# The output projection as seven half-size products instead of eight

## The chip, the cores and the metric

The kernel runs on one core of a Trainium2 chip. The metric is the device time of one execution in microseconds (us). Below, PE is TensorE (matrix products), DVE is VectorE, ACT is ScalarE, POOL is GpSimd and SP is SyncE, which only issues transfers. Each engine works through its own queue in program order; PSUM is the memory that TensorE accumulates into, SBUF the working memory of all engines, DRAM the memory outside.

## The reference

One decoder block on x of 1024 rows by 1024 columns, in float32. Cut to what matters here:

```python
o_a = swa_sink_attention(qa, ka, va, swa_sinks[l])     # sliding window, 8 heads
o_b = mla_attention(q_nope, q_rope, k_nope, k_rope, vb) # causal, 8 heads
y = jax.nn.sigmoid(g_a) * (o_a @ w_o_swa[l]) + jax.nn.sigmoid(g_b) * (o_b @ w_o_mla[l])
x = x + y @ w_out[l]
h = rmsnorm(x, ffn_norm_g[l])
x = x + (jax.nn.silu(h @ w_gate[l]) * (h @ w_up[l])) @ w_down[l]
return rmsnorm(x, final_norm_g)
```

The change concerns `y @ w_out`: 1024x1024 by 1024x1024, with the mixing that makes y ahead of it and the norm and the feed-forward part behind.

## The kernel before

Every float32 operand of a product is split into a rounded upper half and a lower half (`split`, L163 the cast on ScalarE, L166 the subtraction on VectorE), and `mm3` (L172 to L174) makes three matmuls of them: upper by upper, upper by lower, lower by upper. One matmul has a 128x128 stationary tile and 512 columns.

Order of the stages: projections of the input with the sliding-window attention beside them (the gate stage, in which the gates' products run as filler), the second attention, the mixing, the out projection, the feed-forward part, the last norm.

**Mixing.** y is made transposed, in eight bands `dc` of 128 columns, in the order of `DCS`. ScalarE takes the sigmoids of two gates (L1269), GpSimd multiplies the first with the first mixer's projection `ar` (L1434), in two halves of 128x512. TensorE makes the second mixer's projection oB in two halves `sh` (12 matmuls each, one PSUM bank of four of the pool `PX`). VectorE multiplies it with the second gate straight from PSUM (L1420), which frees the bank, adds the two (L180) and splits the sum (`yh` from ScalarE, `yl` from VectorE). All 16 halves are split and stay as `y`. The bands 0 to 3 of `ar` wait in DRAM (`ar_d`). The tile scheduler sets the order here, within the order in which the code was written.

**Out projection.** Four segments (row half `sh`, column half `hf`): (0,0), (0,1), (1,1), (1,0), each of four blocks of 128 rows. One block in one segment is one `xo`: eight bands by three matmuls in a bank of the other PSUM pool `P1`. VectorE adds it to x (L180). The weights come as units of 512 KB ("out", r, j), loaded by SP (L238), split by ScalarE and VectorE; half 0 is loaded and split twice, 12 units in all. After both column halves of a block: Square on ScalarE (L1644), `rstd` on GpSimd (L311, L314), the norm on VectorE (L1649), the block to DRAM, and `to_h`, which transposes it on TensorE and lowers it for the feed-forward part (for blocks 4 to 7 the second half of that, `rest`, is called later). From the last segment on, the order on TensorE, VectorE, ScalarE and GpSimd is that of the code (`manual_schedule`); before, the scheduler's.

**Feed-forward part.** It already works with seven products in place of eight (class `Seven`), its sums made by GpSimd and VectorE. It starts with `ffn.run()`, after loads and sums called `load_part`, `mix` and `prep_to`.

**The gate stage**, where part of the change stands, is a loop of 16 steps; in each GpSimd normalises the sliding window's weights `pe` (L935 to L938), and its loads go through SP.

Of the kernel before, what the change touches and what calls it, by code (L numbers as in the profile page):

```python
# [89 lines left out]
def hybrid_block_kernel(  # L90
# [208 lines left out]
    for dp in range(4):  # L299
        plain(("oa", dp), w_o_swa[dp], (P, 4, 256), True)  # L300
    for dp in (2, 0, 3, 1):
        plain(("ob", dp), w_o_mla[dp], (P, 4, 256))
    OUT0 = (2, 0, 3, 1)
    for r, hf in enumerate((0, 1, 0)):
        for j in (range(4) if r else OUT0):
            plain(("out", r, j), w_out[hf, j], (P, 2, 512), (r, j) != (2, 3))
# [718 lines left out]
    for it in range(N_SW):  # L1025
        if it + 2 < N_SW:
            sw_q(it + 2)
        gate_step()
        if it + 1 < N_SW:
            sw_qT(it + 1)  # L1030
        gate_step()
        if it >= 1:
            sw_pv(it - 1)
        if it + 1 < N_SW:
            sw_scores(it + 1)
        if it == N_SW - 1:
            load_lat(4)
        gate_step()
        sw_pT(it)
# [236 lines left out]
    def mix_a(dc, sh, c0, n, ps=None):  # L1276
        if ps is not None:
            oa_ps[(dc, sh)] = ps
        ps = oa_ps[(dc, sh)]
        if (sh, c0) == (0, 0):  # L1280
            if dc < 4:
                ar[dc] = U("ar")
            elif dc % 2 == 0:
                t = V("ar", F32, (P, 2, S))
                ar[dc], ar[dc + 1] = t[:, 0], t[:, 1]
            if dc % 2 == 0:
                wo[dc // 2] = st.get(("oa", dc // 2))
        w = wo[dc // 2]
        mm3(ps, [((w[0][:, c, blk(dc % 2)], w[1][:, c, blk(dc % 2)]), oaT[(c, sh)]) for c in range(c0, c0 + n)],
            c0 == 0, c0 + n == 4)  # L1290
        if c0 + n == 4:
            nc.scalar.copy(ar[dc][:, half(sh)], oa_ps.pop((dc, sh)))
            if sh == 1 and dc < 4:
                nc.sync.dma_start(ar_d[dc], ar.pop(dc))
# [16 lines left out]
    DCS = (4, 5, 0, 1, 6, 7, 2, 3)  # L1311

    def load_sigs(dc):
        for i in (dc, 8 + dc):
            load_sig(i)
        if dc < 4:
            ar[dc] = U("ar")
            nc.sync.dma_start(ar[dc], ar_d[dc])
# [35 lines left out]
    units = [(u // 2, u % 2, c) for u in range(16 - 3) for c in (0, 2)]  # L1354
# [5 lines left out]
    for t in range(NT):  # L1360
# [20 lines left out]
        if t == NT - 1:  # L1381
            mix_a(13 // 2, 13 % 2, 0, 4, PX("oA"))
# [7 lines left out]
        if t + 6 in w_at or t == 0:  # L1390
            st.load_to(st.index[("oa", w_at.get(t + 6, 0))])
# [6 lines left out]
        if e in (2, 6):  # L1398
            st.load_to(st.index[("ob", 2 if e == 2 else 0)])
        if e == 6:  # L1400
            st.conv_to(st.index[("ob", 2)])
        held[0] = False
    rest = [(i // 2, i % 2) for i in range(14, 16)]
# [6 lines left out]

    def mix_b(dc, i):
# [3 lines left out]
        ga, gb = gate.pop(dc), gate.pop(8 + dc)  # L1415
        for sh in range(2):
# [4 lines left out]
            if i == 7:  # L1421
                add(ga[:, cs], ga[:, cs], gb[:, cs], nc.vector)
                split(*hT(dc, cs), ga[:, cs])
        for sh in range(2 if i < 7 else 0):
            cs = half(sh)
            add(ga[:, cs], ga[:, cs], gb[:, cs], nc.vector)
            split(*hT(dc, cs), ga[:, cs])
# [14 lines left out]
    st.conv_to(st.index[("ob", 0)])  # L1442
    new_quads("y")
    for i, dc in enumerate(DCS):
        if i in (1, 2):
            st.load_to(st.index[("ob", (3, 1)[i - 1])])
        if 2 <= i < 6:
            st.load_to(st.index[("out", 0, OUT0[i - 2])])
# [4 lines left out]
        if i + 1 < 8:  # L1453
            sigmoids(DCS[i + 1])
        mix_b(dc, i)
        if i in (1, 3):
            st.conv_to(st.index[("ob", (3, 1)[i // 2])])
        if i >= 4:
            st.conv_to(st.index[("out", 0, OUT0[i - 4])])

# [3 lines left out]
    x2 = {}  # L1464
# [3 lines left out]
    def to_h(xn, b):  # L1468
# [3 lines left out]
        for kh in range(2):  # L1472
            ps = PX("tp", (P, 4, P))
# [133 lines left out]

    in_order = tc.manual_schedule(engines={engines.PE, engines.DVE, engines.Activation, engines.Pool})
    prev = None
    late_parts = []  # L1610
    for seg, (sh, hf) in enumerate(((0, 0), (0, 1), (1, 1), (1, 0))):
        if seg == 3:
            in_order.__enter__()
        if seg in (0, 1, 3):
            r = {0: 0, 1: 1, 3: 2}[seg]
            wo2 = [st.get(("out", r, j)) for j in range(4)]
        hs = half(hf)
        for b in range(4 * sh, 4 * sh + 4):
            if seg in (0, 2):
                x2[b] = load_x(b)  # L1620
            if (seg, b) == (2, 4):
                ffn.load_part(0, 0)
            if (seg, b) == (2, 6):
                ffn.load_part(0, 1)
            if (seg, b) == (2, 7):
                ffn.mix(0)
            if seg == 0 and b < 2:
                if b == 0:
                    xo2 = [P1("xo") for _ in range(2)]
                    for ks in (DCS[:6], DCS[6:]):  # L1630
                        for u in range(2):
                            mm3(xo2[u], [(hT(k, blk(u)), (wo2[k // 2][0][:, k % 2], wo2[k // 2][1][:, k % 2])) for k in ks],
                                ks[0] == DCS[0], ks[0] != DCS[0])
                ps = xo2[b]
            else:
                ps = P1("xo")
                mm3(ps, [(hT(k, blk(b)), (wo2[k // 2][0][:, k % 2], wo2[k // 2][1][:, k % 2])) for k in DCS])
            add(x2[b][:, hs], ps, x2[b][:, hs], nc.vector)
            if seg in (0, 2):
                st.conv_to(st.index[("out", seg // 2 + 1, b % 4)])  # L1640
            if seg in (1, 3):
                xn = U("xn")
                ss = tiny("ss")
                nc.scalar.activation(xn, x2[b], AF.Square, accum_out=ss)  # L1644
                rs = rstd_of(ss, D)
            lower = to_h(*prev) if prev is not None else None
            prev = None
            if seg in (1, 3):
                nc.vector.scalar_tensor_tensor(xn, x2[b], rs, fg_bc, op0=ALU.mult, op1=ALU.mult)  # L1649
                prev = (xn, b)  # L1650
                if (seg, b) == (3, 6):
                    ffn.prep_to(3)
                nc.sync.dma_start(x2_d[b], x2.pop(b))
            if (seg, b) == (3, 7):
                for kh in range(2):
                    ffn.load_part(1, kh)
            if lower is not None:
                if seg == 3 and b >= 6:
                    late_parts.append(lower)
                else:  # L1660
                    lower()
    ffn.n_ahead = 1
    ffn.run()
    late_parts.pop(0)()
    ffn.run()
    ffn.prep_to(5)
    late_parts.pop(0)()
    ffn.run()
    ffn.prep_to(6)
    lower = to_h(*prev)  # L1670
    ffn.run()
    ffn.run()
    ffn.prep_to(7)
    lower()
# [210 lines left out]
```

## Time and profile before

| | |
|---|---|
| median of 3 runs | 1340.86 us (1339.17 to 1341.85) |
| profiled execution | 1340.2 us, its span 1338.4 us |
| TensorE clock granted | 0.998 |
| TensorE busy | 1325.0 us (99%) |
| VectorE, ScalarE, GpSimd busy | 904.0 (68%), 635.5 (47%), 566.9 us (42%) |
| oB of the mixing on TensorE | from 563.9 us on |
| out projection on TensorE | 607.4 to 699.7 us |

Rows are read as: start, duration, engine, line, operation, output<-inputs, shapes, and in brackets the idle time before it and what ended it. Rows of groups have a count and min/median/max in ns. In rows of stages each engine has its busy time and its number of instructions. A transfer's time to landing is from issue to the last byte.

### The profile page before, as it was taken

What the parts mean: (1) busy time and instruction counts of PE and PEld (TensorE: products, weight loads), DVE (VectorE), ACT (ScalarE), POOL (GpSimd) and SP (SyncE); (2) the same over time, 40 slices, a digit from 0 to 9 for tenths busy, and PEclk for the clock granted to TensorE, in tenths of its full rate; (3) what the DMA queues carried; (4) which work ended last, traced back from release to release, by engine and by line L of the source; (5) the groups of instructions that cost most, each with busy time, mean ns of one, the idle gap of its engine ahead of it and who ended that gap; (6) DMA issues with size and microseconds to landing.
All of it is one profiled execution on the core that took longest, in us unless ns stands there. A gap on an engine that the chain in (4) does not pass through costs nothing. (4 is left out here: it accounts for less than half of the span.)

```text
span 1338.4 us, 19037 instructions
## 1 busy us (share of the span) xinstructions
PE 1325.0 (99%) x6564; PEld 1115.5 (83%) x6564; DVE 904.0 (68%) x1471; ACT 635.5 (47%) x1291; POOL 566.9 (42%) x614
## 2 busy tenths in 40 slices
PE   9999999999999999999999999999999999999997
PEld 6899878888888889888887888888888888888886
DVE  7868777776767766696468766566655564664862
ACT  7434767665557666763436323222233232644443
POOL 2116546553224555451131765756666541022521
PEclk9999999999999999999999999999999999999999
DMA  9455332245476440681533344535543425996504
GB/s 370 158 184 160 114 104 84 100 134 178 161 235 174 95 111 17 240 281 61 212 139 104 144 173 171 198 143 182 181 147 144 170 100 193 386 367 238 173 15 143
DMA packets 85311, 223.61 MB, mean 167 GB/s; under 512 B 9632, under 2 KB 16288, under 8 KB 84128
## 3 DMA queue, kind: packets, MB, share of 16 engines
q1 hardware_dynamic: 83776, 220.05, 47.9%
q10 hardware_dynamic: 1440, 2.36, 0.5%
q8 instruction: 52, 0.85, 0.3%
q14 instruction: 43, 0.35, 0.1%
HBM read 151.72 MB, written 70.12 MB: 166 GB/s over the span
## 5 line engine op out<-in xcount | busy, mean ns | idle before, releaser
L166 DVE TENSOR_TENSOR wl<-wr,wl 128x512 fp32r<-128x512 f32 x150 | 149.3, 1019 | 72.0 <-ACT wl L163 71.7
L166 DVE TENSOR_TENSOR lrv<-lr,lrv 128x1024 fp32r<-128x1024 f32 x77 | 105.2, 1397 | 48.7 <-ACT lrv L163 44.6
L163 ACT CAST lrv<-lr 128x1024 fp32r<-128x1024 f32 x77 | 80.0, 1052 | 95.0 <-PE fd L174 70.1
L172 PE MATMUL fd<-lrv 128*128 128x512 f32 x308 | 119.8, 389 | 0.0
L173 PE MATMUL fd<-lrv 128*128 128x512 f32 x308 | 119.8, 389 | 0.0
L174 PE MATMUL fd<-lrv 128*128 128x512 f32 x308 | 119.8, 389 | 0.0
L177 POOL TENSOR_TENSOR wr<-wr,sm 128x512 f32<-128x512 f32 (+1 forms) x38 | 46.6, 1234 | 145.8 <-DVE wl L166 115.5
L163 ACT CAST wl<-wr 128x512 fp32r<-128x512 f32 x150 | 87.0, 623 | 1.8 <-DVE wr L835 1.5
L1198 POOL TENSOR_TENSOR denb<-denb,neg_one 128x1 f32<-128x1 f32 x64 | 40.1, 626 | 96.2 <-ACT p L1197 84.0
L166 DVE TENSOR_TENSOR wl<-sm,wl 128x512 fp32r<-128x512 f32 x60 | 49.0, 844 | 46.4 <-ACT wl L163 46.2
L173 PEld LDWEIGHTS fd<-lrv 128*128 128x128 f32 x308 | 57.8, 188 | 12.1
L172 PEld LDWEIGHTS fd<-lrv 128*128 128x128 f32 x308 | 57.8, 188 | 12.0
L174 PEld LDWEIGHTS fd<-lrv 128*128 128x128 f32 x308 | 57.8, 188 | 11.8
L311 POOL TENSOR_SCALAR ms<-ss 128x1 f32<-128x1 f32 x32 | 8.5, 266 | 138.1 <-ACT xn L1644 61.0
L1197 ACT ACTIVATE p<-scb,nmb 128x384 f32<-128x384 f32 (+3 forms) x64 | 47.8, 747 | 33.3 <-DVE nmb L1196 25.6
L166 DVE TENSOR_TENSOR ptl<-pTb,pth 128x512 fp32r<-128x512 f32 (+2 forms) x96 | 50.5, 552 | 16.6 <-ACT pth L163 16.3
L1196 DVE CUSTOM_DVE_ANT_0 scb<-scb,mask 128x384 f32<-128x384 f32 (+3 forms) x64 | 48.6, 762 | 15.0 <-PE scb L1188 13.0
L1529 ACT ACTIVATE act<-sm 128x512 f32<-128x512 f32 x11 | 7.0, 634 | 104.4 <-DVE sm L180 104.4
L1199 POOL TENSOR_SCALAR p<-p,denb 128x384 f32<-128x384 f32 (+3 forms) x64 | 47.9, 748 | 6.3
L1529 ACT ACTIVATE act<-pu 128x512 f32<-128x512 f32 x22 | 13.9, 633 | 70.8 <-DVE pu L180 70.8
L163 ACT CAST pth<-pTb 128x512 fp32r<-128x512 f32 (+2 forms) x96 | 43.4, 482 | 8.5 <-PE pTb L1213 7.5
L172 PE MATMUL fb<-t2h,wl 128*128 128x512 f32 x120 | 47.4, 395 | 0.0
(356 smaller groups left out, 4318.0 us busy)
## 6 DMA issues: line engine op xcount, KB each, us to landing
lr<-la_d SPq DMA_DIRECT2D x77, 256.0 KB, 5.4
wr<-in_w_gate_dram SPq DMA_DIRECT2D x22, 512.0 KB, 4.2
wr<-in_w_up_dram SPq DMA_DIRECT2D x22, 512.0 KB, 5.2
wd<-in_w_down_dram SPq DMA_DIRECT2D x22, 512.0 KB, 7.2
rb_d<-wd SPq DMA_DIRECT2D x22, 512.0 KB, 2.7
la_d<-sd SPq DMA_DIRECT2D x22, 512.0 KB, 5.7
lr<-rb_d SPq DMA_DIRECT2D x44, 256.0 KB, 5.4
lr<-in_w_down_dram SPq DMA_DIRECT2D x33, 256.0 KB, 5.2
```

The source lines that it names most:

```text
L163: i = nc.scalar.copy(hi, src)
L166: (eng or nc.vector).tensor_tensor(lo, src, hi.bitcast(F32), op=ALU.subtract)
L172: nc.tensor.matmul(ps, ah, bh, start=first and i == 0, stop=False, skip_group_check=go_on)
L173: nc.tensor.matmul(ps, ah, bl, start=False, stop=False, skip_group_check=go_on)
L174: nc.tensor.matmul(ps, al, bh, start=False, stop=last and i == n - 1, skip_group_check=go_on)
L177: eng.tensor_tensor(out, a, b, op=ALU.subtract)
L311: nc.gpsimd.tensor_scalar(ms, ss, 1.0 / width, EPS, op0=ALU.mult, op1=ALU.add)
L1196: nc.vector.tensor_tensor_reduce(s_, s_, m_, 1.0, -NEG, op0=ALU.add, op1=ALU.min, accum_out=nm)
L1197: nc.scalar.activation(p_, s_, AF.Exp, scale=-1.0, bias=nm, accum_out=den)
L1198: nc.gpsimd.tensor_tensor(den, den, neg_one[:, 0:1], op=ALU.pow)
L1199: nc.gpsimd.tensor_scalar(p[:, 0:w], p[:, 0:w], den, 0.0, op0=ALU.mult, op1=ALU.add)
L1529: nc.scalar.activation(dst, src, AF.Silu)
```

## The change

With the rows of y in halves a (0) and b (1), its columns in halves, and w_out in four quarters b11, b12, b21, b22, the product is made as seven products of half size q = 1 to 7, in the order 1, 2, 5, 6, 3, 7, 4, each in four blocks `xo(q, b)` of 12 matmuls: 336 matmuls in place of 384. Each has a left operand of `y` sums and a right operand of weight sums.

- **Weight sums** t1 to t4 are made in DRAM in the gate stage (`out_sums`): SP copies a quarter, or an earlier sum, DRAM to DRAM (four copies of 1 MB), and GpSimd issues four transfers that add to it (`accum_op`). Their units of 512 KB are loaded as before, 14 of them; for q = 6 the split negates.
- **Row sums** are made in SBUF (`left_sum`): 16 accumulating transfers of 128x512, four for each of four band pairs k, issued by GpSimd. Within a pair each uses the result of the one before, and GpSimd's queue waits for it. The bands from 4 on are stored negated (L1473, one instruction for product and sum), so that sums serve as differences.
- **Splits**: 12 halves are split in the mixing stage and 16 more sums later (`split_left`), 28 in place of 16. The mixed bands `ya` stay in SBUF until then.
- **Banks**: products 1, 6, 7, 4 accumulate in banks of `PX`, products 2, 5, 3 in `P1`; each is added to or subtracted from x when it stands, 28 additions in place of 16. The first ones, xo(1, b), take the four `PX` banks of the last four oB. The transposes of blocks 0 to 3 move to `P1`.
- **Order**: `DCS` is (0,1,4,5,2,3,6,7), the `ar` bands from 4 on wait in DRAM, and the loads of weights follow. The order of the four engines is that of the code from xo(1,0) on.

```diff
+    def out_unit(q, u):
...
+        def conv(raw):
+            hi, lo = halves_of((P, 2, 512), True)
+            if q == 6:
+                a = nc.scalar.activation(hi, raw, AF.Copy, scale=-1.0)
+                nc.vector.scalar_tensor_tensor(lo, raw, -1.0, hi.bitcast(F32), op0=ALU.mult, op1=ALU.subtract)
+            else:
+                split(hi, lo, raw)
...
+    def more(dst, src, **kw):
+        nc.gpsimd.dma_start(dst, src, accum_op=ALU.add, **kw)
+    def out_sums(i):
...
+        if i == 0:
+            nc.sync.dma_start(t1, b11)
+            nc.sync.dma_start(t3, b22)
+        if i == 2:
+            more(t1, b12, max_dma_last_dim=4096)
+            more(t3, b12, max_dma_last_dim=4096)
+        if i == 4:
+            nc.sync.dma_start(t2, t1)
+        if i == 6:
+            more(t2, b22, max_dma_last_dim=4096)
+        if i == 8:
+            nc.sync.dma_start(t4, t2)
+        if i == 10:
+            more(t4, b21, max_dma_last_dim=4096)
...
     for it in range(N_SW):
         if it + 2 < N_SW:
             sw_q(it + 2)
+        out_sums(it - 1)
         gate_step()
...
-    DCS = (4, 5, 0, 1, 6, 7, 2, 3)
+    DCS = (0, 1, 4, 5, 2, 3, 6, 7)
...
+        def mixed(sh):
+            cs = half(sh)
+            if dc < 4:
+                add(ga[:, cs], ga[:, cs], gb[:, cs], nc.vector)
+            else:
+                nc.vector.scalar_tensor_tensor(ga[:, cs], ga[:, cs], -1.0, gb[:, cs], op0=ALU.mult, op1=ALU.subtract)
+            if dc >= 4 or sh == 0:
+                hi, lo = left[1 if dc < 4 else 2 if sh == 0 else 4]
+                split(hi[:, dc % 4], lo[:, dc % 4], ga[:, cs])
...
+    def left_sum(n, *ks):
+        for k in ks:
+            a_lo, a_hi, b_lo, b_hi = (ya[k + d][:, half(sh)] for d in (0, 4) for sh in range(2))
+            more(*{0: (b_hi, a_hi), 1: (a_hi, a_lo), 2: (a_lo, b_hi), 3: (b_lo, a_lo)}[n])
+    def split_left(q, *ks):
+        if q not in left:
+            new_left(q)
+        d, sh = {5: (4, 1), 7: (0, 1), 6: (0, 0), 3: (4, 0)}[q]
+        for k in ks:
+            split(left[q][0][:, k], left[q][1][:, k], ya[k + d][:, half(sh)])
...
+    SUMS = {4: [(0, 0)], 5: [(0, 1), (1, 0)], 6: [(1, 1), (2, 0)], 7: [(2, 1), (3, 0)]}
...
+        for n, k in SUMS.get(i, ()):
+            left_sum(n, k)
...
-            ps = PX("tp", (P, 4, P))
+            ps = (P1 if b < 4 else PX)("tp", (P, 4, P))
...
+    def xo(q, b):
+        if q in (1, 2, 5):
+            bank[("B" if q == 1 else "A", b)] = (PX if q == 1 else P1)("xo")
+        ps = bank[("B" if q in (1, 6, 7, 4) else "A", b)]
+        w = [st.get(("out", q, u)) for u in range(2)] if b == 0 else wop[q]
+        wop[q] = w
+        lh, ll = left[q]
+        mm3(ps, [((lh[:, k, blk(b)], ll[:, k, blk(b)]), (w[k // 2][0][:, k % 2], w[k // 2][1][:, k % 2]))
+                 for k in range(4)], first=q in (1, 2, 5), go_on=q in (6, 7, 4, 3))
+        x_ = x2[b if q in (1, 2, 6, 3) else 4 + b][:, lo if q in (1, 2, 4) else hi]
+        if q in (1, 5, 7):
+            add(x_, ps, x_, nc.vector)
+        else:
+            sub(x_, x_, ps, nc.vector)
...
+    left_sum(0, 2, 3)
+    left_sum(1, 2, 3)
+    left_sum(2, 2, 3)
+    left_sum(3, 1, 2, 3)
+    xo(1, 0)
...
+    xo(7, 1)
+    to_h_of(1)
+    conv(4, 1)
+    ffn.load_part(0, 1)
+    xo(4, 0)
+    norm_b(3)
+    norm_a(4)
+    to_h_of(2)
...
+    xo(4, 3)
+    norm_a(7)
+    norm_b(6)
+    to_h_of(5)
...
     ffn.n_ahead = 1
     ffn.run()
-    late_parts.pop(0)()
+    lowers.pop(4)()
+    ffn.prep_to(4)
+    to_h_of(6)
     ffn.run()
+    lowers.pop(5)()
     ffn.prep_to(5)
-    late_parts.pop(0)()
+    to_h_of(7)
     ffn.run()
```

GpSimd in the mixing stage, before: the multiplications of the eight bands (sg is a gate's tile, ar the first mixer's).

```order
300 L1434 TENSOR_TENSOR sg_6455<-ar_5796,sg_6455 128x512 x2
301 L1434 TENSOR_TENSOR sg_6589<-ar_5796,sg_6589 128x512 x2
302 L1434 TENSOR_TENSOR sg_6614<-ar_6618,sg_6614 128x512 x2
303 L1434 TENSOR_TENSOR sg_6674<-ar_6678,sg_6674 128x512 x2
304 L1434 TENSOR_TENSOR sg_6726<-ar_6373,sg_6726 128x512 x2
305 L1434 TENSOR_TENSOR sg_6770<-ar_6373,sg_6770 128x512 x2
306 L1434 TENSOR_TENSOR sg_6818<-ar_6822,sg_6818 128x512 x2
307 L1434 TENSOR_TENSOR sg_6867<-ar_6871,sg_6867 128x512 x2
```

The same place after, from the fourth band's multiplication on.

```order
307 L1505 TENSOR_TENSOR sg_6676<-ar_6680,sg_6676 128x512 x2
308 L328 DMA sg_6618<-sg_6467 128x512
309 L1505 TENSOR_TENSOR sg_6725<-ar_6385,sg_6725 128x512 x2
310 L328 DMA sg_6467<-sg_6467 128x512
311 L328 DMA sg_6467<-sg_6618 128x512
312 L1505 TENSOR_TENSOR sg_6773<-ar_6385,sg_6773 128x512 x2
313 L328 DMA sg_6676<-sg_6600 128x512
314 L328 DMA sg_6618<-sg_6467 128x512
315 L328 DMA sg_6600<-sg_6600 128x512
316 L1505 TENSOR_TENSOR sg_6820<-ar_6824,sg_6820 128x512 x2
317 L328 DMA sg_6600<-sg_6676 128x512
318 L1505 TENSOR_TENSOR sg_6868<-ar_6872,sg_6868 128x512 x2
```

Seven transfers now stand between the last five pairs of multiplications; rows 308, 310, 311 and 314 are the chain of the first band pair, 313, 315 and 317 that of the second.

VectorE at the seventh band, before: multiplication of oB, lower halves (yl), sums (sg from two sg), a weight's lower half (wv).

```order
904 L1420 TENSOR_TENSOR sg_6820<-oB_6918,sg_6820 128x512
905 L166 TENSOR_TENSOR yl_6613<-sg_6770,yh_6612 128x512
906 L180 TENSOR_TENSOR sg_6818<-sg_6818,sg_6820 128x512
907 L166 TENSOR_TENSOR wv_6989<-wr_6865,wv_6989 128x1024
908 L1420 TENSOR_TENSOR sg_6820<-oB_6932,sg_6820 128x512
909 L166 TENSOR_TENSOR yl_6607<-sg_6818,yh_6606 128x512
```

And after.

```order
903 L1482 TENSOR_TENSOR sg_6822<-oB_6921,sg_6822 128x512
904 L1473 SCALAR_TENSOR_TENSOR sg_6820<-sg_6820,sg_6822 128x512
905 L166 TENSOR_TENSOR yl_6734<-sg_6820,yh_6733 128x512
906 L1482 TENSOR_TENSOR sg_6822<-oB_6935,sg_6822 128x512
907 L1473 SCALAR_TENSOR_TENSOR sg_6820<-sg_6820,sg_6822 128x512
```

Between the band's two multiplications of oB stand the sum of its first half (which reads what GpSimd has multiplied) and that half's split, where a sum, a weight's and an older half's split stood.

ScalarE in the projection, before: the copies and casts (hraw, b11h, b21h) that take a block's transposes out of PSUM, and casts of weights (wv, wh) in the third segment.

```order
677 L163 CAST wv_7357<-wr_7355 128x1024
678 L1483 COPY hraw_7370<-tp_7360 128x512
679 L163 CAST b11h_7206<-tp_7360 128x4x128
680 L1483 COPY hraw_7370<-tp_7365 128x512
681 L163 CAST b21h_7208<-tp_7365 128x4x128
682 L163 CAST wv_7407<-wr_7405 128x1024
683 L163 CAST wv_7444<-wr_7442 128x1024
684 L163 CAST wh_7485<-wr_7483 128x1024
```

After, ahead of xo(4,0): Square of block 3, the cast of the unit (4,0), block 1's transposes, the cast of the unit (4,1).

```order
686 L1712 ACTIVATE xn_7447,ss_7448<-x_7007 128x1024
687 L163 CAST wv_7454<-wr_7355 128x1024
688 L1559 COPY hraw_7480<-tp_7470 128x512
689 L163 CAST b11h_7404<-tp_7470 128x4x128
690 L1559 COPY hraw_7480<-tp_7475 128x512
691 L163 CAST b21h_7406<-tp_7475 128x4x128
692 L163 CAST wv_7487<-wr_7357 128x1024
693 L1712 ACTIVATE xn_7509,ss_7510<-x_7112 128x1024
```

The last weights were converted during the third segment, ahead of the segment that uses them; now each of the two casts stands just ahead of the product that reads it.

More of the change, by code (lines that the diff above doesn't have):

```diff
@@ new lines, in hybrid_block_kernel @@
+    lo, hi = half(0), half(1)
+    bank = {}
+    normed = {}
+    lowers = {}
+    def xo(q, b):
[12 more added lines that the diff above has]
+            sub(x_, x_, ps, nc.vector)
+        if b == 3:
+            left.pop(q)
+            wop.pop(q)
@@ new lines, in hybrid_block_kernel @@
+    xo(2, 0)
+    split_left(5, 3)
+    x2[4] = load_x(4)
+    x2[5] = load_x(5)
+    xo(2, 1)
+    conv(6, 0)
+    x2[6] = load_x(6)
+    x2[7] = load_x(7)
+    xo(2, 2)
+    conv(6, 1)
+    ahead(3, 1)
+    xo(2, 3)
+    split_left(6, 0, 1)
+    xo(5, 0)
+    split_left(6, 2, 3)
+    xo(5, 1)
+    conv(3, 0)
+    xo(5, 2)
+    conv(3, 1)
+    ahead(7, 1)
+    xo(5, 3)
+    split_left(3, 0, 1)
+    xo(6, 0)
+    split_left(3, 2, 3)
+    xo(6, 1)
+    split_left(7, 0, 1)
+    xo(3, 0)
+    norm_a(0)
```

198 lines of the change are left out of this document (112 added, 86 removed).

## The prediction

> **What bounds the kernel now.** I read the page first, then the stages around the out projection, then who waited for whom, and last the single instructions on VectorE and GpSimd.
>
> ```profile
> span 1338.4 us, 19037 instructions
> PE 1325.0 (99%) x6564; PEld 1115.5 (83%) x6564; DVE 904.0 (68%) x1471; ACT 635.5 (47%) x1291; POOL 566.9 (42%) x614
> q1 hardware_dynamic: 83776, 220.05, 47.9%
> q10 hardware_dynamic: 1440, 2.36, 0.5%
> q8 instruction: 52, 0.85, 0.3%
> q14 instruction: 43, 0.35, 0.1%
> ```
>
> TensorE is busy 99% of the span, so a removed product pays in full if nothing takes its place, and any new wait of TensorE costs in full. The queue table has no queue fed from GpSimd: the price of an accumulating transfer has no row here.
>
> ```profile
> 564.00:608.00 44.00, 44.00 (x196) 36.45 (x195) 39.82 (x45) 28.89 (x35) 23.67 (x14) 1.00 0.84 303
> 608.00:680.00 72.00, 72.00 (x336) 59.94 (x335) 37.66 (x44) 24.66 (x38) 15.06 (x16) 1.00 0.30 119
> 680.00:700.00 20.00, 20.00 (x98) 16.68 (x97) 13.29 (x18) 8.11 (x15) 2.85 (x6) 1.00 0.33 122
> 700.00:720.00 20.00, 19.84 (x95) 16.01 (x94) 17.35 (x25) 11.39 (x20) 4.04 (x4) 1.00 0.31 108
> PE fa L172 <- ACT wl L163: 0.2, 1, 0.2
> PE fa L172 <- ACT pu L812: 0.2, 1, 0.2
> ```
>
> The first four rows are stages (length; then busy time of TensorE, weight load, VectorE, ScalarE, GpSimd; clock; DMA share; GB/s): mixing (564 to 608), the out projection, and the start of the feed-forward part. The last two are every wait of TensorE between 555 and 725: 0.4 us. In the mixing stage VectorE works 39.8 of 44 us and the DMA engines 0.84 of the time; from 608 to 700 VectorE has 41 of 92 us free, from 700 on 2.6 of 20.
>
> **What the change removes.** 384 products of 128x512 become 336.
>
> ```profile
> L172 PE MATMUL oB<-obT,wh x64: 389/389/389, 563.9 to 606.7; 128*128 128x512 f32 x64
> L172 PE MATMUL xo<-wv,yh x120: 389/389/478, 607.4 to 699.2; 128*128 128x512 f32 x120
> ```
>
> Each lasts 389 ns but they overlap: the 64 of the first row, every third of a run of 192, start 42.8 us apart from first to last, so 42.8/(63 x 3) = 0.227 us each. 48 fewer save 48 x 0.227 = 10.9 us. (48 x 0.389 = 18.7 would price the overlap twice.) A block's product now has 12 matmuls, 2.72 us, where it had 24, 5.45. The transposes stay.
>
> **What it adds in the gate stage.** Four plain copies on SP's queue and four accumulating transfers on GpSimd's sum the weights in DRAM, over 400 us before their use.
>
> ```profile
> 592.07 0.33 SPq L329 DMA_DIRECT2D x<-in_x_dram  x1
> 161.47 0.20 POOL L935 TENSOR_TENSOR den<-den,es 128x4 f32<-128x4 f32 x1 [2.16 <-ACT pe L933]
> 171.98 0.20 POOL L935 TENSOR_TENSOR den<-den,es 128x4 f32<-128x4 f32 x1 [3.81 <-ACT pe L933]
> ```
>
> SP spends 0.33 us on an issue. GpSimd starts each step of that stage after a wait for ScalarE, 2.16 and 3.81 us in these steps 10.5 apart, so at most two issues per step fit in idle time. I take 0 (ends 0 and 1.5, the issues of three steps were the idle time gone).
>
> **What it adds in the mixing stage.** This is the largest term, since GpSimd's queue is in order and holds, between the multiplications that the mixing needs, transfers that wait for each other.
>
> ```profile
> 589.75 3.45 POOL L1434 TENSOR_TENSOR sg<-ar,sg 128x512 f32<-128x512 f32 x2 [5.08 <-DVE sg L1420]
> 610.21 3.45 POOL L1434 TENSOR_TENSOR sg<-ar,sg 128x512 f32<-128x512 f32 x2 [4.70 <-ACT sg L1269]
> 606.58 0.68 DVE L1420 TENSOR_TENSOR sg<-oB,sg 128x512 f32<-128x512 f32 x1
> 607.18 0.68 DVE L166 TENSOR_TENSOR yl<-sg,yh 128x512 fp32r<-128x512 f32 x1
> 609.52 0.68 DVE L1420 TENSOR_TENSOR sg<-oB,sg 128x512 f32<-128x512 f32 x1
> 610.72 1.78 DVE L180 TENSOR_TENSOR sg<-sg,sg 128x512 f32<-128x512 f32 x1
> 616.16 0.69 DVE L1420 TENSOR_TENSOR sg<-oB,sg 128x512 f32<-128x512 f32 x1
> L163 ACT CAST yh<-sg x16: 600/621/627, 570.5 to 617.7; 128x512 fp32r<-128x512 f32 x16
> L166 DVE TENSOR_TENSOR yl<-sg,yh x16: 676/692/1780, 572.1 to 618.3; 128x512 fp32r<-128x512 f32 x16
> ```
>
> Let L be the time from a transfer's issue to its landing. What GpSimd spends on issuing one has no row: between SP's 0.33 and one of its own multiplications, 3.45 / 2 = 1.73, I take 1.0. The fifth round's multiplications end at 589.75 + 3.45 = 593.2, as before. Then the order on GpSimd gives: second transfer of chain 0 at 593.2, third at 593.2 + L, sixth round's multiplications from 594.2 + L to 597.7 + L, first transfer of chain 1 there, its successor when that has landed, at 597.7 + 2L, seventh round's multiplications from 598.7 + 2L. VectorE follows in order: half of that pair (1.73), the negating sum, the cast on ScalarE (0.62), the lower half (0.69), and then the multiplication (0.68) that frees the PSUM bank. For the sum I take 1.78, since it stands beside the pair's second half as the sum at 610.72 stood beside the pair at 610.21 (0.68 is the low end). So the bank is free at 604.2 + 2L. The projection's second product xo(1,1) takes it and is due at 607.4 + 2.72 = 610.1: a wait of 2L - 5.9. The same way the eighth round stands behind the third transfer of chain 1 (597.7 + 3L) and frees the bank of xo(1,3), due at 615.6, at 604.2 + 3L: together 3L - 11.4 where that is more. In the kernel before these multiplications came at 609.52 and 616.16 and nobody waited: its projection started on four other banks.
>
> For L the nearest rows:
>
> ```profile
> gate_d<-go SPq DMA_DIRECT2D x32, 256.0 KB, 2.1
> lr<-rb_d SPq DMA_DIRECT2D x44, 256.0 KB, 5.4
> wr<-in_w_out_dram SPq DMA_DIRECT2D x5, 512.0 KB, 5.9
> DMA to landing us min/median/max: 5.3/6.5/7.5
> ```
>
> The third row is the window 585 to 609 alone, the fourth the four x loads of 512 KB issued there. An accumulating transfer of 128x512 moves 256 KB but reads 256 KB from both sides, in the stretch in which the DMA engines are 0.84 busy. So 2.1 (a store in a quiet stage) is the lower end and 7.5 the upper; I take 6.5, the median of transfers with as many bytes read, in the same stretch. Wait: 3 x 6.5 - 11.4 = 8.1 us (ends: 0, and 11.1). The remaining transfers land before they are read up to an L of about 7; beyond that the left-hand sums are late too, by my estimate some 3 us at 8.
>
> On the length of L the Trainium skill, "DMA: Bandwidth & Descriptors" (Anatomy of one DMA), fits a GpSimd-issued transfer as 2.0 us plus bytes over 436 GB/s, by estimate 2.6 us for 256 KB. By it the term would be 0 and the whole sum -4.7 us; no run here shows such a transfer.
>
> **What it adds in the projection.** Twelve more additions of products and twelve more lower halves of 0.69, 16.6 us, against VectorE's 41 us free between 608 and 700: hidden, apart from three places with rows here.
>
> ```profile
> 640.27 0.69 DVE L180 TENSOR_TENSOR x<-xo,x 128x512 f32<-128x512 f32 x1 [1.33 <-PE xo L174]
> 641.00 1.06 ACT L1644 ACTIVATE xn<-x 128x1024 f32<-128x1024 f32 x1 [4.29 <-DVE x L180]
> 642.05 0.57 ACT L1483 COPY hraw<-tp 128x512 f32<-128x512 f32 x1
> 643.47 0.61 ACT L163 CAST b21h<-tp 128x512 fp32r<-128x512 f32 x1
> 646.62 0.69 DVE L180 TENSOR_TENSOR x<-xo,x 128x512 f32<-128x512 f32 x1 [0.62 <-PE xo L174]
> 606.62 1.05 ACT L163 CAST wv<-wr 128x1024 fp32r<-128x1024 f32 x1
> 608.38 1.21 DVE L166 TENSOR_TENSOR wv<-wr,wv 128x1024 fp32r<-128x1024 f32 x1
> ```
>
> First, xo(4,0). Its two weight units are converted late. From T, the end of xo(3,3): addition and Square until T + 1.95 (as 640.27 to 642.05, after 0.2), cast of the first unit until T + 3.0, its lower half T + 4.2; four copies of the transposes that run at T + 2.7, until T + 5.2 (642.05 to 643.47 + 0.61 is four of them); cast of the second unit T + 6.2; lower half T + 7.4. TensorE arrives at T + 2.72 + 0.89 = T + 3.6 (eight transposes take 0.89: the additions at 640.27 and 646.62 lie 6.35 apart, with 24 matmuls or 5.45 between). It waits 0.4 for the first lower half, 0.9 for the second cast, 1.0 for its lower half: 2.3 us.
>
> Second, the last transposes. Between the end of xo(4,3) and the second bank of block 7's transposes TensorE has 24 matmuls and 20 transposes, 5.45 + 2.25 = 7.7 us. VectorE has 13 short instructions, 0.60 apart (606.58 to 607.18), and two of 1.22 there, 10.4 us, and ScalarE's copy of 0.59 follows: 3.3 us more than TensorE can fill.
>
> Third, the first feed-forward products, with the lowerings of blocks 4 to 7 now all between them: before's waits there were 0.4, VectorE has 2.6 of 20 us to spare; 0.4 to 2, I take 1.0.
>
> VectorE's free time can also shrink, as in the sum of 1.78 us above. After 619 GpSimd multiplies nothing in the projection, so I take none of that. Here the Trainium skill, "SBUF — State Buffer" (the "DVE blocks DMA" trap), speaks against the change: descriptors of a GpSimd-issued transfer are not written while VectorE holds the shared port, 0.62 us becoming 3.1. The rows agree as far as the two engines slow each other. With 3.1 us instead of 1.0 for each of the two issues that stand ahead of the seventh round, by estimate, the sum would be some 4 us higher.
>
> **Sum.** -10.9 + 0 + 8.1 + 2.3 + 3.3 + 1.0 - 0.4 (before's own waits) = +3.4 us on the profiled run's 1340.2, thus 1343.6; that run stands 0.7 under the median of 1340.86, so 1344.3 by the median, and I say 1344.
>
> **Rivals.** The projection's terms, 6.2 with before's waits taken off, leave 4.7 of gain for the mixing to eat. A: short landing. At L of 3.9 or less the mixing costs at most 2.0 and the sum is -2.7 to -4.7: 1336 to 1338, faster. For it: stores land in 2.1. Against: every x load in that stretch took 5.3 or more. It decides at that L. B: everything hidden, the full 10.9: 1330. For it: VectorE's 41 free us. Against: ScalarE's order puts the second unit's cast behind four copies. C: long landing, L of 8 or more: 3 x 8 - 11.4 = 12.6 plus 3 for the late sums, in all +10.9: 1352. For it: 7.5 was seen, and transfers of one chain cannot overlap. Against: most loads there are shorter. D: no difference, with L from 3.9 to 6.2, or with a longer L and half of the projection's waits hidden: 1338.2 to 1343.5.
>
> **How the numbers follow.** 0.2%, 2.7 us, is about what a measurement of this kernel can tell from no change. The forecast (L of 6.2 to 8, slower, 1343.5 to 1350) has 0.35, C 0.17, D 0.20, A 0.20, B 0.08. Faster is A and B, 0.28; same is D, 0.20; slower the forecast and C, 0.52. The range leaves out B and the far part of C: 1333 to 1354.
>
> **What would show it.** A queue fed from GpSimd appears, and its transfers' issue-to-landing is L. GpSimd's seventh pair of multiplications starts at 598.7 + 2L. TensorE waits for VectorE's multiplication of oB at about 611 to 618, for the cast and lower half of a weight in xo(4,0), and in the last transposes. The out projection's matmuls take 336 x 0.227 = 76.3 us. I am wrong if the first of these waits is absent (L under 3), if the casts come early enough to make the projection tight, or if the gate stage becomes longer. The predicted median is 1344 us.

## The result

The changed kernel takes 1352.55 us (median of 4 runs, 1348.26 to 1354.29), against 1340.32 (1339.17 to 1341.85) for the kernel before, measured beside it: a ratio of 1.0079, 95% interval 1.0062 to 1.0097. It is slower, as forecast, but by 12 us where I had said 3.4. The profiled run is the fastest of the four, 1348.26 us with a span of 1346.5. Its span is 8.1 us longer than that of before, and the accounts below are of these 8.1 us; of the other 4 a second profile tells more (run 2). Runs are called by their numbers in the list of experiments.

From the page of the changed kernel (the span, the busy times, the queue fed from GpSimd) and from the groups of TensorE's waits (total us, how often, the longest; 3.1 us of groups that are the same in the kernel before are left out):

```profile
span 1346.5 us, 19053 instructions
PE 1320.1 (98%) x6516; PEld 1107.7 (82%) x6516; DVE 926.6 (69%) x1497; ACT 644.2 (48%) x1305; POOL 577.5 (43%) x634
q0 software_dynamic: 3392, 8.39, 3.5%
PE xo L172 <- DVE sg L1482: 2.3, 2, 1.9
PE tp L1551 <- ACT t L1568: 2.3, 2, 1.7
PE fa L172 <- ACT wl L163: 2.0, 2, 1.1
PE oB L172 <- DVE sg L1482: 1.9, 1, 1.9
PE pT L993 <- POOL pe L981: 1.8, 1, 1.8
PE kvq L565 <- DMA wr<-in_w_x_dram: 1.4, 1, 1.4
PE tp L1551 <- DVE xn L1717: 1.3, 1, 1.3
PE xo L173 <- DVE wv L166: 1.2, 2, 0.8
PE xo L172 <- ACT wv L163: 0.6, 1, 0.6
PE fa L172 <- ACT pu L855: 0.3, 2, 0.2
PE fa L174 <- DVE wl L166: 0.3, 1, 0.3
```

TensorE has 48 matmuls fewer (6564 to 6516). Two numbers of the page give the account. Its idle time (span less busy) went from 1338.4 - 1325.0 = 13.4 us to 26.4: 13.0 more. Its busy time fell by only 4.9 us, where 48 x 0.227 = 10.9 were taken out: what is left ran 6.0 us longer. So 13.0 + 6.0 - 10.9 = 8.1.

The idle time is in the list above, nearly all of it. In the gate stage `pT` waits 1.8 for GpSimd. In the mixing stage and the first half-size products `oB` and `xo` wait 1.9 + 2.3 for VectorE's multiplications. In `xo(4,0)` the waits for `wv` are 1.2 + 0.6, in the last transposes `tp` has 2.3 + 1.3, and at the first feed-forward products there are 0.6 us. (The 2.0 for `wl` stood in before too. The first product waits 1.4 for its weights, where before it waited 0.2 for them and 0.5 for ScalarE; this changes from run to run, 0.4 to 1.9 us in the profiles below, and no experiment is about it.)

Of the 6.0 us of longer work, 3.4 are found in two stretches behind those waits (length; busy times of TensorE, weight load, VectorE, ScalarE, GpSimd; granted clock; DMA share; GB/s). Two single matmuls of the first one follow:

```profile
604.80:608.20 3.40, 3.40 (x9) 2.65 (x8) 3.30 (x6) 0.46 (x2) 0.88 (x1) 0.50 0.95 253
707.20:710.60 3.40, 3.40 (x11) 2.82 (x12) 3.40 (x4) 1.34 (x3) 0.78 (x1) 0.50 0.01 4
604.25 0.50 PE L172 MATMUL oB<-obT,wv 128*128 128x512 f32 x1 [1.93 <-DVE sg L1482]
605.26 0.63 PE L172 MATMUL oB<-obT,wv 128*128 128x512 f32 x1
```

Behind the wait of 1.93 us, and again among the waits of the transposes, the granted clock is 0.50 for 3.4 us. Half of the clock for 3.4 us is 1.7 us lost, nearly as much as the wait itself; the kernel before has no such stretch up to 1330 us. The other 2.6 us are not placed by a row. Part of them is that a matmul ahead of a wait lasts its 0.389 us where the next one would have started after 0.227: with about 10 new waits that is 1.6 us by my estimate. Up to the first `oB` matmul nothing runs longer: TensorE is busy 557.8 us there in both kernels, and the shift of 2.9 us (563.9 to 566.8) is idle time alone.

### The profile page after: what moved, and what is told of

Read it like the earlier page. It is cut to its first block, busy times and chain, and to the rows that moved or that the text cites. A ratio compares the mean times of both kernels' runs of the same rounds, so it can differ in the third digit from the quotient of the medians.

```text
span 1346.5 us, 19053 instructions
## 1 busy us (share of the span) xinstructions
PE 1320.1 (98%) x6516; PEld 1107.7 (82%) x6516; DVE 926.6 (69%) x1497; ACT 644.2 (48%) x1305; POOL 577.5 (43%) x634
## 5 line engine op out<-in xcount | busy, mean ns | idle before, releaser
L1605 ACT ACTIVATE act<-pu 128x512 f32<-128x512 f32 x22 | 13.9, 633 | 71.1 <-DVE pu L180 71.1
```

What stands on the lines that cost most here:

```text
L1605: nc.scalar.activation(dst, src, AF.Silu)
```

## What GpSimd's queue looks like now

GpSimd's rows in the gate stage of the changed kernel, and the matmul that waited:

```profile
158.44 1.12 POOL L328 DMA_DIRECT2D wt_d<-in_w_out_dram  x1
168.66 0.92 POOL L328 DMA_DIRECT2D wt_d<-in_w_out_dram  x1 [9.11 <-issue]
169.28 0.53 POOL L978 TENSOR_TENSOR den<-den,es 128x4 f32<-128x4 f32 x1
171.56 1.69 PE L993 MATMUL pT<-ident,pe 128*128 128x128 f32 x4 [1.75 <-POOL pe L981]
```

The second transfer stands right behind the first. GpSimd was idle for 9.11 us ahead of it, and nothing that the profile shows ended that time; the first took about as long to land (9.7 us is the median of the two). The softmax normalisation (`den`, `pe`) is queued behind it, and TensorE waits for that.

In the mixing stage, GpSimd's rows around the sixth to eighth pair of multiplications, then three of VectorE's:

```profile
597.88 0.86 POOL L328 DMA_DIRECT2D sg<-sg  x1 [3.01 <-DMA sg<-sg]
598.45 2.85 POOL L1505 TENSOR_TENSOR sg<-ar,sg 128x512 f32<-128x512 f32 x2
602.28 0.90 POOL L328 DMA_DIRECT2D sg<-sg  x1 [0.98 <-DVE yl L166]
605.97 0.88 POOL L328 DMA_DIRECT2D sg<-sg  x1 [2.79 <-DMA sg<-sg]
608.21 0.87 POOL L328 DMA_DIRECT2D sg<-sg  x1 [1.35 <-DMA sg<-sg]
608.78 2.88 POOL L1505 TENSOR_TENSOR sg<-ar,sg 128x512 f32<-128x512 f32 x2
614.93 0.89 POOL L328 DMA_DIRECT2D sg<-sg  x1 [3.28 <-DMA wr<-wt_d]
615.56 2.80 POOL L1505 TENSOR_TENSOR sg<-ar,sg 128x512 f32<-128x512 f32 x2
```

```profile
598.79 3.08 DVE L166 TENSOR_TENSOR yl<-sg,yh 128x512 fp32r<-128x512 f32 x1
608.68 3.53 DVE L166 TENSOR_TENSOR yl<-sg,yh 128x512 fp32r<-128x512 f32 x1
616.09 2.83 DVE L166 TENSOR_TENSOR yl<-sg,yh 128x512 fp32r<-128x512 f32 x1 [0.74 <-ACT yh L163]
```

The transfers wait for each other's landing, as the prediction had it, and the pairs of multiplications behind them come late. But there is a second effect. Before, an instruction of VectorE that met such a pair lasted 1.78 us: it got in after the first of the two multiplications. Here a pair with a transfer's issue right ahead of it holds the instruction until both are through, 2.8 to 3.5 us in these rows. The Trainium skill, "SBUF — State Buffer" (SBUF: two separate sides), states that the port which the two engines share is locked for a whole instruction; in these rows VectorE's instruction is held for two. The rows show that it is held, and not the port.

## The experiments

The first eight edits were run beside kernels before of 1340.24 or 1340.02 us (medians); ratios are to those.

**1. The weight sums alone.** The kernel before, with `out_sums` and its call added and its result left unused; nothing else of the change.

```diff
     for it in range(N_SW):
...
+        out_sums(it - 1)
         gate_step()
```

> The kernel before with the weight sums of the gate stage added (four copies by SyncE, four accumulating transfers by GpSimd) and used by nothing: the projection stays at eight products. Theory: those transfers alone cost the gate stage what the changed kernel lost there, because the second accumulating transfer was issued 9.1 us late and GpSimd's normalisation stood behind it: 1342.5 to 1344, with TensorE waiting some 1.8 us for GpSimd in the gate stage and the first oB near 566.5 instead of 563.9. Rival (the 2.9 us there come from loads that landed later by chance): 1339.5 to 1341.5 and no such wait.

1344.22 us (1342.59 to 1348.71, 8 runs), ratio 1.0029 (1.0019 to 1.0040); span 1342.1, 3.7 more than before. GpSimd's queue and TensorE:

```profile
158.20 1.09 POOL L309 DMA_DIRECT2D wt_d<-in_w_out_dram  x1
168.43 0.92 POOL L309 DMA_DIRECT2D wt_d<-in_w_out_dram  x1 [9.13 <-issue]
171.33 2.70 PE L975 MATMUL pT<-ident,pe 128*128 128x128 f32 x8 [2.00 <-POOL pe L963]
171.40:174.80 3.40, 3.36 (x11) 2.33 (x12) 1.94 (x3) 2.59 (x8) 3.32 (x7) 0.50 1.04 195
```

The stage costs 4 us by itself, with the same 9.1 us ahead of the second issue. The wait is 2.00 us, and behind it the clock is 0.50 for 3.4 us again, 1.7 us more: together the 3.7 of the span.

**2. The second transfer a step later.**

```diff
             more(t1, b12, max_dma_last_dim=4096)
+        if i == 3:
             more(t3, b12, max_dma_last_dim=4096)
```

> The changed kernel with the two accumulating transfers of one step of the gate stage put into two successive steps. Theory: the wait of 9.1 us in front of the second goes, TensorE's 1.8 us wait for GpSimd with it, and the first oB starts near 564 to 565: 2 to 3 us faster than the changed kernel, 1349.5 to 1350.5. Rival: the transfer is late wherever it stands, no change.

1351.85 us (1351.45 to 1354.07), ratio 1.0086 (1.0071 to 1.0101). The scheduler put the transfer right behind the first again: GpSimd's idle time ahead of it was 9.16 us and TensorE waited 2.18. The edit did not move what it was meant to move, so it tells nothing of either theory.

It tells something else. All five queues hold the instructions of the changed kernel in the same order, so this is a second profile of that kernel, of an execution of 1354.07 us:

```profile
L172 PE MATMUL oB<-obT,wv x64: 389/389/497, 571.6 to 617.0; 128*128 128x512 f32 x64
177.30:180.70 3.40, 3.40 (x10) 2.62 (x9) 2.05 (x4) 1.02 (x3) 3.22 (x6) 0.50 0.67 131
```

Its span is 13.9 us longer than that of before, and the first `oB` matmul starts 7.7 us later, where the first profile had 2.9. From the gate stage's first transposition `pT` to that matmul the kernel before takes 415.5 us, the first profile of the changed one 418.7, and this one 421.7, with 0.50 of the clock behind the wait. Runs 4 to 7 have the same instructions up to there and take 419.5 to 423.2. So the profile behind "The result" is of the execution that lost least in the gate stage: the stage costs 3.2 to 7.7 us, and from the first `oB` matmul to the end the two profiles are only 1.0 us apart (779.7 and 780.7, before 774.5).

**3. Fewer, longer rows.** The same bytes, as 128 rows of 8 KB in place of 256 of 4 KB.

```diff
-        return t.rearrange("j p k c -> (j p) (k c)")
+        return t.rearrange("j (p r) k c -> (j p) (r k c)", r=2)
...
-            more(t1, b12, max_dma_last_dim=4096)
+            more(t1, b12, max_dma_last_dim=8192)
```

> The changed kernel with the four accumulating transfers of the weight sums cut into 128 rows of 8 KB instead of 256 rows of 4 KB: the same bytes, half the pieces. Theory (GpSimd's second transfer of the step waits because the queue has no room for its pieces while the first is under way; 3 transfers of 128 pieces each were issued back to back in the projection): the wait of 9.1 us goes, TensorE's wait for GpSimd with it, and the 3.9 us that the weight sums cost the kernel before fall to under 1: about 1349. Rival (the second waits for the first to land, or for the copy into its target): the wait stays, about 1352.

1355.99 us (1354.24 to 1357.21), ratio 1.0114 (1.0099 to 1.0129), slower where 1349 was expected. GpSimd issues both in 1.91 us and the normalisation follows, but TensorE then waits elsewhere:

```profile
160.74 1.91 POOL L328 DMA_DIRECT2D wt_d<-in_w_out_dram  x2
162.96 0.20 POOL L978 TENSOR_TENSOR den<-den,es 128x4 f32<-128x4 f32 x1 [0.31 <-ACT pe L976]
176.64 0.51 ACT L880 ACTIVATE wr<-wr,gT 128x256 f32<-128x256 f32 x1 [7.98 <-DMA wr<-in_w_gt_dram]
180.94 0.79 PE L172 MATMUL fb<-t3h,wl 128*128 128x512 f32 x1 [5.36 <-ACT wl L163]
wt_d<-in_w_out_dram POOLq DMA_DIRECT2D x2, 1024.0 KB, 11.9
wr<-in_w_gt_dram SPq DMA_DIRECT2D x3, 512.0 KB, 11.6
```

So the 9.1 us hung on the form of the transfer: two of 256 rows do not stand in the queue together, two of 128 do. (Number and length of the rows changed together.) And with both in flight a load of the gate's weights took 11.6 us to land (the last two rows are the window 140 to 185), against 3.7 in the same window of the kernel before. ScalarE waited 8 us for it, TensorE 5.4. In the changed kernel, with the same copies by SP but one of the two transfers behind the other, the same load has a median of 5.9 us: the overlap of the two goes with the longer landing.

**4. The row sums behind the mixing loop.** All 16 `left_sum` transfers are written behind the loop.

```diff
     for i, dc in enumerate(DCS):
...
-        for n, k in SUMS.get(i, ()):
-            left_sum(n, k)
...
-    left_sum(0, 2, 3)
+    left_sum(0, 0, 1, 2, 3)
...
```

> The changed kernel with all 16 row sums issued after the last multiplication of the mixing, by kind instead of by band pair, so that no multiplication stands behind a transfer. Theory (multiplications behind chained transfers hold back VectorE, which frees the PSUM banks): TensorE's waits for VectorE's multiplication of oB, 4.2 us in all, go, and with them the slow clock of 1.6 us after the first of them: 5 to 6 us faster than the changed kernel, about 1347. Rival 1 (VectorE itself is the bound in the mixing, whatever GpSimd does): most of the 4.2 us stay. Rival 2: the sums land too late, and TensorE waits the same time for split sums in the products 5 to 3.

1350.58 us (1348.45 to 1352.86), ratio 1.0068 (1.0051 to 1.0085), where about 1347 was expected. `xo` no longer waited for a multiplication and no sum was late, but `oB` waited 3.3 us in place of 1.9. Two transfers still stood between the pairs, since the scheduler raised them. That gives a comparison within one run, GpSimd's row first in each pair of rows:

```profile
594.87 0.96 POOL L328 DMA_DIRECT2D sg<-sg  x1 [6.48 <-DVE yl L166]
595.57 2.84 POOL L1505 TENSOR_TENSOR sg<-ar,sg 128x512 f32<-128x512 f32 x2
...
608.21 3.43 POOL L1505 TENSOR_TENSOR sg<-ar,sg 128x512 f32<-128x512 f32 x2 [1.49 <-ACT sg L1313]
```

```profile
595.26 3.71 DVE L1473 SCALAR_TENSOR_TENSOR sg<-sg,sg 128x512 f32<-128x512 f32 x1
608.71 1.79 DVE L180 TENSOR_TENSOR sg<-sg,sg 128x512 f32<-128x512 f32 x1
```

With a transfer's issue right ahead of the pair VectorE is held 3.71 us, without one 1.79, and the first of these transfers waited for no other. So the hold does not come from the landing times.

**5. The same, with GpSimd's order held.** The pairs and the transfers behind them keep the order of the code.

```diff
+            if len(pins) > 6:
+                tc.keep_in_program_order(pins[-1])
...
-            more(*{0: (b_hi, a_hi), ...
+            tc.keep_in_program_order(more(*{0: (b_hi, a_hi), ...
```

> As the run with the sums after the mixing, but with the order on GpSimd held, so that no transfer at all stands between its multiplications (there, two still did, and VectorE's one instruction of 3.7 us came right behind one of them). Theory (a transfer issued right ahead of a pair of multiplications makes VectorE wait for the whole pair, 2.8 to 3.7 us instead of 1.8): no VectorE instruction over 2.4 us between 566 and 620, TensorE's waits for VectorE's multiplication of oB fall from 4.2 us to under 1.3, and the kernel is 4 to 6 us faster than the changed one: 1346.5 to 1348.5. Rival (VectorE's order, each half's sum, split and next multiplication one after the other with 0.7 us for the cast, is what holds TensorE): waits of 2 us and more stay.

1347.16 us (1346.83 to 1348.27), ratio 1.0050 (1.0035 to 1.0065), 5.4 us under the changed kernel. In the mixing stage and the first products TensorE has one wait:

```profile
609.89 0.50 PE L172 MATMUL oB<-obT,wv 128*128 128x512 f32 x1 [2.12 <-DVE sg L1482]
626.01 2.69 POOL L328 DMA_DIRECT2D sg<-sg  x3 [4.84 <-DVE yl L166]
```

In this stage no VectorE instruction lasts longer than 2.4 us any more, and the waits at `xo` and at the fourteenth `oB` product are gone. But the fifteenth now waits 2.1 us, which the theory had not foreseen: of 4.2 us of waits half went. By the profiles, the stretch from the first `oB` matmul to the end takes 777.3 us in place of 779.7 (780.7 in run 2), so 2.4 to 3.4 us are this edit's; the rest of the 5.4 is not shown to be.

**6. The second unit of `xo(4,0)` converted earlier.**

```diff
+    conv(4, 1)
     xo(7, 1)
     to_h_of(1)
-    conv(4, 1)
```

> The changed kernel with the conversion of the last weight unit (4,1) moved ahead of xo(7,1) and of block 1's transposes. Theory: of the three waits in xo(4,0), 0.47, 0.58 and 0.76 us, the last two go: 1.3 us faster than the changed kernel, about 1351. Rival: the copies of the transposes come later instead, and TensorE waits at the next transposes: no change.

1349.19 us (1348.01 to 1351.28), ratio 1.0064 (1.0049 to 1.0079). Of the three waits of `xo(4,0)`, 1.8 us, one of 0.5 is left. That confirms where they came from; the intervals of this kernel and the changed one overlap, so the gain itself is shown by the waits and not by the times.

**7. A lighter end.** One subtraction of each lowering on GpSimd, and the last lowering one feed-forward product later.

```diff
-        sub(r[:, 1], r[:, 1], t23[:, 0], nc.vector)
+        sub(r[:, 1], r[:, 1], t23[:, 0], nc.gpsimd)
...
-    to_h_of(7)
     ffn.run()
+    to_h_of(7)
```

> The changed kernel with two edits behind the projection: of the lowering of blocks 4 to 7 the second difference, which nothing needs soon, on GpSimd instead of VectorE, and the transposes of block 7 one feed-forward product later. Theory (VectorE has more to do there than TensorE's work covers): of TensorE's waits at the transposes, 3.5 us, the one at block 7 (1.66) goes and the slow clock after them (0.86 over 12 us, 1.7 us) shrinks: 2 to 3.5 us faster, 1349 to 1350.5. Rival (GpSimd's instructions hold up VectorE's by as much as they take off it): no change.

1351.70 us (1347.97 to 1355.02), ratio 1.0073 (1.0055 to 1.0092). The transposes' wait for ScalarE fell from 2.3 to 0.6 us, the 1.3 for `xn` stayed at 1.4, and the first feed-forward products waited 0.3 more. By the time no gain shows.

**8. Edits 3, 5, 6 and 7 together.**

> All edits at once: the weight sums in 8 KB rows, the row sums behind the mixing in held order, the last weight converted earlier, the second differences on GpSimd and block 7's transposes one product later. If the causes add up: 1352.5 - 3 - 5 - 1.3 - 2.8 = 1340.4, near the kernel before; waits of 4 to 5 us against 10.9 saved would give 1334 to 1336. If the mixing keeps its waits: 1344 to 1346.

1347.19 us (1346.65 to 1348.41), ratio 1.0050 (1.0035 to 1.0065): the causes did not add up to the 1340.4 expected. The gate stage keeps the 5.4 us wait of edit 3, and its first `oB` matmul starts at 571.6, 7.7 us later than before. From the first `xo` matmul to the end it takes 725.5 us, where the kernel before takes 731.0.

**9. The weight sums in the second attention.** As 8, with the copies and transfers held at one place in each head.

```diff
     for t in range(NT):
...
+        if n == NB - 1:
+            out_sums(2 * h)
         if t + 2 < NT:
             scores(t + 2)
```

> This is the kernel with all four edits (1347.2 us, gate stage 7.7 us later than before at the first of the mixing stage's products), with the six transfers that make the weight sums taken out of the gate stage and held in the second attention, one accumulating transfer a head, where GpSimd has a gap of about 4 us in each head and the weights are wanted only from about 609 us. Theory (the gate stage is what is left of the loss; nothing else in the change needs it): the 7.7 us come back, the first of the mixing stage's products starts within 0.7 us of before (563.9), and the time is 1347.2 - 7.7 = 1339.5, band 1338.5 to 1341.5. Rival (any large accumulating transfer on GpSimd costs the stage it stands in): the softmax multiplications that GpSimd does for the second attention are held up, TensorE shows new waits between 400 and 560 us, and the time stays at 1343 to 1347.

1339.83 us (1338.64 to 1342.26, 11 runs) against 1341.48 (1339.42 to 1344.06, 21 runs): ratio 0.9994 (0.9985 to 1.0003), so no difference from the kernel before, and 7.4 us less than run 8. In the second attention a transfer stands in GpSimd's gap, and no new wait of TensorE there is over 0.6 us:

```profile
431.35 0.59 POOL L1242 TENSOR_SCALAR p<-p,denb 128x384 f32<-128x384 f32 x1
431.88 1.05 POOL L328 DMA_DIRECT2D wt_d<-in_w_out_dram  x1
435.95 0.56 POOL L1241 TENSOR_TENSOR denb<-denb,neg_one 128x1 f32<-128x1 f32 x1 [3.02 <-DVE ptl L166]
PE oB L172 <- DVE sg L1483: 2.4, 2, 2.1
PE tp L1554 <- DVE xn L1720: 1.4, 1, 1.4
```

The first `oB` matmul is at 565.0, 1.1 us later than before and not the 0.7 that I had allowed. The last two rows are the largest waits left between 560 and 725 us.

**10. The second product's weights converted later**, to clear VectorE in the rounds of that 2.1 us wait.

```diff
-        if i >= 4:
-            st.conv_to(st.index[("out", 1 + i // 6, i % 2)])
+        if i in (4, 5):
+            st.conv_to(st.index[("out", 1, i % 2)])
...
     xo(1, 0)
+    conv(2, 0)
+    xo(1, 1)
+    conv(2, 1)
+    xo(1, 2)
     conv(5, 0)
```

> The kernel before in this list, with the conversion of the second product's weights moved from the last rounds of the mixing stage to behind the first half-size products (those of the fifth one product later too), to take 1.2 to 2.3 us of VectorE out of the rounds in which TensorE waited 2.1 us for a multiplication. Theory (VectorE's load in the last rounds, one operation held by a pair of GpSimd's, makes that wait): the 2.1-us wait goes, with some 0.5 us of slower clock behind it, and the time is 2 to 3 us under the kernel before in this list: 1336.5 to 1338.5 if that one comes out at 1339.5. Rival (the pair of GpSimd's alone holds VectorE, or the conversions come too late where they now stand): the wait stays or moves to the first half-size products, and the two times are within 0.7 us of each other.

("The kernel before in this list" is number 9.) 1340.04 us (1338.22 to 1341.98, 11 runs), ratio 0.9989 (0.9980 to 0.9998). The wait is gone:

```profile
PE xo L173 <- DVE wv L166: 0.7, 2, 0.5
PE xo L174 <- DVE yl L166: 0.5, 2, 0.4
PE oB L172 <- DVE sg L1483: 0.3, 1, 0.3
```

So VectorE's load made that wait. But the time is that of number 9, as the rival had it: `xo` and the feed-forward products wait 0.5 and 0.8 us longer. From the first `oB` matmul to the end the two profiles are 0.8 us apart (772.1 and 772.9). Both are within 0.2% of the kernel before.

## Why the prediction was right on the sign and short on the size

The prediction's sum was 3.4 us on the profiled run; that run shows 8.1, and the medians lie 12 apart. The median of 1352.55 is beyond the 1343.5 to 1350 of the forecast itself, at the price of rival C (1352), whose landings of 8 us or more the profiled run does not have (3.4 to 7.5).

| term | predicted, us | in the profile after, us |
|---|---|---|
| products removed | -10.9 | -10.9 by count |
| gate stage | 0 (0 to 1.5) | 3.2, of it 1.75 waiting for GpSimd; 6.2 in run 2's profile; 3.7 of the span alone (run 1) |
| mixing: waits | 8.1 | 1.93 + 0.39 + 1.92 = 4.2 |
| xo(4,0) | 2.3 | 0.47 + 0.58 + 0.76 = 1.8 |
| last transposes | 3.3 | 1.27 + 0.61 + 1.66 = 3.5 |
| first feed-forward products | 1.0 | 0.6 |
| longer work of the matmuls left | not in the sum | 6.0, of it 3.4 at half of the clock |

**The sign was in part luck.** With the waits that were measured, the prediction's own terms make -10.9 + 4.2 + 1.8 + 3.5 + 0.6 - 0.4 = -1.2 us: a kernel a little faster. It is slower by two costs that the sum had at nothing, the gate stage and the clock, while the term that made the sum positive was half as large.

**The step that failed is the gate stage taken at 0.** It counted issues ("at most two issues per step fit in idle time") and priced each at 0.33 to 1.7 us. An issue did take 0.9 to 1.1 us there. What was not thought of is that the second could not be issued while the first was under way: 9.1 us in which GpSimd stood still in front of work that TensorE needs. Run 1 shows that step alone, run 3 that it hung on the rows of the transfer, and run 9 that the stage's cost goes when the transfers leave it. The prediction had named "if the gate stage becomes longer" as one way to be wrong.

**A cost is missing from the sum: the clock after a wait.** Each new wait was priced at its length. The rows at 604.8 and 707.2 show another 1.7 us behind each of two groups of them. The 6.0 us of longer work are more than the whole forecast.

**The mixing term had the right mechanism and was too large.** The seven transfers among the multiplications landed in 3.5, 3.6, 7.5, 5.3, 7.3, 6.4 and 6.2 us, where I took 6.5 for all. With the ones on which the pairs waited, 3.6, 5.3 and 6.4, the sum of L is 15.3 and the term 15.3 - 11.4 = 3.9 us, against 4.2 measured. The seventh pair would start at 598.7 + 3.6 + 5.3 = 607.6, plus 2.9 for the late gate stage 610.5; it started at 608.78. The wait at xo(1,1) is there, 1.92, and the one expected at xo(1,3) is not; a bank earlier, at `oB`, there is another of 1.93. That one stands behind the second effect, which the prediction had taken at the 1.78 of an undisturbed pair: VectorE held for the whole pair. In run 5, without the hold, it is gone, and the next product waits as long for a VectorE that has too much to do (run 10). After 619 GpSimd multiplies nothing, as said, and no such hold is seen.

By the fit in the Trainium skill, "DMA: Bandwidth & Descriptors" (Anatomy of one DMA), 256 KB would land in an estimated 2.6 us. No accumulating transfer of this kernel landed in under 3.4. Rival A needed an L of 3.9 or less, which the first two of the mixing stage had and the other five did not. The other price that the prediction named, 3.1 us for an issue, was not seen: the seven issues among the multiplications took 0.86 to 0.96.

**The end of the projection came out as reckoned**, term by term within 0.5 us. (In the term for the last transposes 13 x 0.60 + 2 x 1.22 is 10.2, not 10.4, so the reckoning should have given 3.1.) Runs 6 and 7 took causes away one at a time, and most of these waits went with them; the one for `xn` stayed.

Rival B, everything hidden, did not come about in any run. In run 9 no transfer stands among the multiplications and none in the gate stage, and the casts come earlier. Even then the 10.9 us of removed products buy a time within 0.2% of before, as 6.6 us of new idle time (1337.9 - 1317.9 = 20.0 against 13.4) and 3.8 of longer work take them up. Whether the waits left in the transposes can be hidden too wasn't tried.

## What to carry to other kernels

A transfer issued from a compute engine's queue can cost that engine more than its issue: ask what is queued behind it if it cannot be issued, and put it where that engine has a gap and nobody waits on the next thing. On a kernel in which TensorE is 99% busy, price a removed product at its pitch, a new wait at its length and the slower matmuls behind it, and expect several small waits to use up a gain of under one per cent. When one profile is the fastest of several executions, look for a second one before dividing up the loss (run 2). Where an edit leaves the order to a scheduler, read the order it made before reading the time (runs 2 and 4).

## What was not expected of the hardware

- Two accumulating transfers of 1 MB in 256 rows were issued 10.2 us apart, with 9.1 us of idle queue; in 128 rows both went out in 1.91 us (run 3), and three of 128x512 in 2.69 (run 5).
- After a wait of 1.93 us the granted clock was 0.50 for 3.4 us, with matmuls of 0.63 us in place of 0.39; after one of 2.00 in run 1 and one of 2.18 in run 2 it was the same 0.50 for 3.4 us, and after one of 2.01 in run 4 for 6.8 us. After 1.75 us in the gate stage of the changed kernel (1.00 from 148 to 200) and after 2.29 in run 5 (1.00 from 171 to 200) it did not fall. So the length of the wait alone does not decide it; what does stays open.
- A pair of GpSimd multiplications right behind a transfer's issue ran in 2.8 to 2.9 us and held one VectorE instruction for 2.8 to 3.7; in the kernel before, without the issue, the pairs that met such an instruction took 3.4 to 3.6 us and held it 1.78.
- Accumulating transfers of 256 KB within SBUF took 3.4 to 7.5 us to land in the profiled run.
